# One-hots an expert ahead in bf16 and expert weights in chunk order, in a transformer block with expert-choice routing

## The chip, the cores and the metric

One core of a Trainium2 chip runs the whole block in one launch. The engines are TensorE (PE; its weight loads are listed as PEld), VectorE (DVE), ScalarE (ACT), GpSimd (POOL) and SyncE (SP, which here only issues transfers). The metric is the time of one execution on the device in microseconds. Three runs of the kernel before gave 1910.66, 1912.56 and 1914.64 us; their median is 1912.56 us.

## The reference

A diffusion-transformer block on 1024 tokens of width 1024, with 256 context tokens. It normalises and modulates the tokens, projects them, runs two attentions of 8 heads each (one over all tokens from a compressed latent, one over a local window), gates, projects and normalises again. Behind that comes the part that the change touches, a layer of 16 experts in which each expert chooses its tokens:

```
aff = softmax(u @ w_router)                  # 1024 tokens x 16 experts
g, idx = top_k(aff.T, 128)                   # each expert takes its 128 best tokens
xe = u[idx]                                  # 16 x 128 x 1024
h  = silu(xe @ w_exp_gate) * (xe @ w_exp_up) # 1024 x 1024 matrices per expert
ye = (h @ w_exp_down) * g
moe = zeros.at[idx].add(ye)                  # back to the tokens
out = layer_norm(ALPHA * x + g2 * moe)
```

Inputs and result are f32. The weights of the experts are 16 x 3 x 4 MB.

## The kernel before

Everything runs in an order written out by hand; each engine works through its instructions in that order and waits on semaphores. The attention, the projections and the normalisations come first and are left as they are. The expert stage begins at about 1206 us of the trace.

Each expert is a list of 12 chunks of weights (`units`, L1197): gate and up for two halves f of the hidden width and two halves q of the model width, then four chunks of down. A chunk is 1 MB and lies in one slot of a ring of 17 (`RB`, `slot_of_ring`); `load_next` (L1206) issues the next transfer on the SP queue as soon as a chunk has been used up. The source of a gate or up chunk is a block of 512 x 512 of the weight matrix, so a partition's 8 KB come as four runs of 2 KB; a down chunk comes as two runs of 4 KB.

To keep the precision of f32 with fast matmuls, each half chunk (128 x 1024) is split into a rounded high part on ScalarE (L1688) and the remainder on VectorE (L1689), at most four halves ahead of TensorE (`split_ahead`). Each product is then three matmuls of 512 columns (`mm3`, L90 to L92): 144 per expert. The expert's tokens and its hidden activations are transposed on TensorE in four groups of four 128 x 128 blocks (`transposed`, L1623) and split too (L1630, L1631). Expert 0 uses four of its chunks whole, in f32 matmuls (L1703).

The routing is done beside expert 0. `jobs` (from L1705) hangs small pieces of work on a place (expert, chunk i, quarter k). From the affinities come a threshold per expert (`highest`, `tau0` to `tau2`), masks and prefix sums (`pick0` to `pick2`), and then `slot`: for each token and expert its place among the expert's 128, or a value above 128.

To turn places into a list of tokens, the kernel builds one-hot matrices. For expert e and each of the 8 groups of 128 tokens, GpSimd compares a row 0..127 with the token's place (`onehot`, L1570); a 128 x 128 one-hot as the stationary operand, times a table `vals` of 17 f32 columns (token number and the 16 affinities), summed over the 8 groups in PSUM, gives each place its token and its gate (`summed`, L1575). There is room for four one-hots (`oh4`), so the work is in two parts:

```
def gather0(e):                      # at quarter k=0 of the chunk
    summed(found[e], oh4, vals, 0)
    onehot(slot[:, :, e], 4)
def gather1(e):                      # at quarter k=3
    summed(found[e], oh4, vals, 4)
    listed(e)                        # VectorE casts, GpSimd fetches the rows of u2
    if e < E - 1:
        onehot(slot[:, :, e + 1], 0)
```

`listed` (L1579) casts the sums to an index and a gate on VectorE (L1582, L1584) and starts an indirect transfer that fetches the 128 token rows (L1465). Expert 1's list is made in expert 0 (`onehot1`, `gather_first`, all 8 one-hots on VectorE), the lists of experts 2 and 3 in expert 1, and from then on the list of expert e in expert e - 2, at its chunk 2. At the end of an expert VectorE scales the output (L1787) and GpSimd adds it to the tokens' rows in memory by an indirect transfer (L1792). Beside expert 14, `order0` to `order2` work out an order of the rows for the end with the same one-hots. Behind the experts follow a normalisation and the output.

Of the kernel before, what the change touches and what calls it, by code (L numbers as in the profile page):

```python
# [9 lines left out]
F32 = mybir.dt.float32  # L10
F32R = mybir.dt.float32r
I32 = mybir.dt.int32
BF16 = mybir.dt.bfloat16
AF = mybir.ActivationFunctionType
OP = mybir.AluOpType
AX = mybir.AxisListType

T, L, D, H = 1024, 256, 1024, 8
N = T + L
KT = 8  # L20
E, CAP = 16, 128
# [6 lines left out]
def block_kernel(ctx, tc, a, out, dbg=None):  # L28

    nc = tc.nc  # L30
# [145 lines left out]
    with ExitStack() as st:  # L176
# [76 lines left out]
        for i in range(1, 4):  # L253
            k = 2 * i - 2
# [107 lines left out]
    o = {}  # L362
# [639 lines left out]
    with ExitStack() as st:  # L1002
# [39 lines left out]
        slot = kp.tile([128, 8, E], F32, name="slot")  # L1042
        col = kp.tile([128, 1], F32, name="col")
        flip = kp.tile([128, 128], F32, name="flip")
        onesr = kp.tile([128, 128], F32R, name="onesr")
        onesb = kp.tile([128, 128], BF16, name="onesb")
        idx0 = kp.tile([128, 1], I32, name="idx0")
        gg0 = kp.tile([128, 1], F32, name="gg0")
        gt = kp.tile([128, 9, E], F32R, name="gt")
        eq = kp.tile([128, 9, E], F32R, name="eq")  # L1050
        utr = kp.tile([128, 128], F32R, name="utr")
        er = kp.tile([128, 8, E], F32, name="er")
        tau = kp.tile([128, E], F32, name="tau")
        top = kp.tile([32, 128], F32, name="top")
        oh4 = kp.tile([128, 4, 128], F32, name="oh4")
        w0 = oh4[0:32].rearrange("p t c -> p (t c)")
        nst = ctx.enter_context(ExitStack())
        np_ = pool(nst, "rows", side="right")
        wr = np_.tile([128, KT, 32], F32, name="wr")
# [29 lines left out]
        def router():  # L1089
# [12 lines left out]
            lambda: rowload(sh2b, mod_d, 1),  # L1102
            lambda: (rowload(sc2b, mod_d, 2), nc.gpsimd.tensor_scalar(sc2b, sc2b, 1.0, None, op0=OP.add)),
            lambda: (nc.sync.dma_start(flip, a["flip"]), router()),
            lambda: (nc.sync.dma_start(col, a["col"]), nc.gpsimd.tensor_copy(onesr, ones),
                     nc.gpsimd.tensor_copy(onesb, ones)),
            lambda: (nc.gpsimd.memset(gt.bitcast(F32), 0.0), nc.gpsimd.memset(eq.bitcast(F32), 0.0),
                     nc.gpsimd.tensor_copy(utr, ut)),
        ]
        mhl, wo = {}, {}  # L1110
# [68 lines left out]
    def y_tile():  # L1179
        return xyp.tile([128, D], F32, name="ye")  # L1180
# [25 lines left out]
    def load_next(queue=nc.sync):  # L1206
        if pos[0] >= len(stream):
            return
        e, w, f, q = stream[pos[0]]
        raw = slot_of_ring()  # L1210
        if w == "down":
            r0 = f * 512 + q * 256
            src = a["w_exp_down"][e, r0:r0 + 256, :].rearrange("(k p) c -> p k c", p=128)
            queue.dma_start(raw.rearrange("p (k c) -> p k c", k=2), src)
        else:
            src = a["w_exp_" + w][e, q * 512:(q + 1) * 512, f * 512:(f + 1) * 512].rearrange("(k p) c -> p k c", p=128)
            queue.dma_start(raw.rearrange("p (k c) -> p k c", k=4), src)
        raws.append(raw.rearrange("p (k c) -> p k c", k=4))

    with ExitStack() as st:  # L1220
# [266 lines left out]
    with ExitStack() as st:  # L1487
# [7 lines left out]
        def bank(tag):  # L1495
            return psm.tile([128, 512], F32, name=tag)
# [45 lines left out]
        def prefix(m, q, first):  # L1542

            v = q.rearrange("p (t e) -> p t e", e=E)
            nc.tensor.matmul(v, utr, m, start=first, stop=False, skip_group_check=True)
            for t in range(8):
                nc.tensor.matmul(v[:, t + 1:9], onesr, m[:, t:t + 1].to_broadcast([128, 8 - t, E]),
                                 start=False, stop=(t == 7), skip_group_check=True)
            return v

        def pick1():
            q = bank("pY")
            vg = prefix(gt, q[:, 0:9 * E], True)
            vq = prefix(eq, q[:, 256:256 + 9 * E], False)
            nc.vector.tensor_copy(tau, vg[:, 8])
            nc.vector.tensor_tensor(er, vq[:, 0:8], tau[:, None, :].to_broadcast([128, 8, E]), op=OP.add)
            nc.vector.tensor_scalar(er, er, float(CAP), None, op0=OP.is_lt)
            eqf, gtf = eq.bitcast(F32)[:, 0:8], gt.bitcast(F32)[:, 0:8]
            nc.vector.tensor_tensor(er, er, eqf, op=OP.mult)
            nc.vector.tensor_tensor(gt[:, 0:8], gtf, er, op=OP.add)  # L1560

        def pick2():
            vs = prefix(gt, bank("pY")[:, 0:9 * E], True)
            nc.vector.tensor_scalar(er, gt.bitcast(F32)[:, 0:8], -1024.0, 1024.0, op0=OP.mult, op1=OP.add)
            nc.vector.tensor_tensor(slot, vs[:, 0:8], er, op=OP.add)

        def onehot(col, t0):

            for t in range(4):
                nc.gpsimd.tensor_scalar(oh4[:, t], iot, col[:, t0 + t:t0 + t + 1], None, op0=OP.is_equal)  # L1570

        def summed(pi, oh, what, t0):

            for t in range(t0, t0 + 4):
                nc.tensor.matmul(pi, oh[:, t - t0], what[:, t], start=(t == 0), stop=(t == 7))  # L1575

        found = {}

        def listed(e):  # L1579
            pi = found.pop(e)  # L1580
            idx = p.tile([128, 1], I32, name="idx", bufs=4)
            nc.vector.tensor_copy(idx, pi[:, 0:1])  # L1582
            gg = p.tile([128, 1], F32, name="gg", bufs=4)
            nc.vector.tensor_copy(gg, pi[:, 1 + e:2 + e])  # L1584
            xe = x_tile() if e % 2 else xe0
            fetch(xe, idx)
            got[e] = idx, gg, xe

        def gather0(e):
            found[e] = bank("pY")[:, :1 + E]  # L1590
            summed(found[e], oh4, vals, 0)
            onehot(slot[:, :, e], 4)

        def gather1(e):
            summed(found[e], oh4, vals, 4)
            listed(e)
            if e < E - 1:
                onehot(slot[:, :, e + 1], 0)

        ohs = []  # L1600

        def onehot1():
            oh = y_tile().rearrange("p (t c) -> p t c", c=128)
            nc.vector.tensor_tensor(oh, iot[:, None, :].to_broadcast([128, 8, 128]),
                                    slot[:, :, 1:2].to_broadcast([128, 8, 128]), op=OP.is_equal)
            ohs.append(oh)

        def gather_first():
            found[1] = bank("pY")[:, :1 + E]
            for t in (0, 4):  # L1610
                summed(found[1], ohs[0][:, t:], vals, t)
            listed(1)
            onehot(slot[:, :, 2], 0)

        def pair_of_parts():
            return [p.tile([128, 4, 128], F32R, name=n, bufs=3) for n in ("xh", "xl")]
# [95 lines left out]
        jobs[0, 7, 1] = [tau2]  # L1712
        jobs[0, 7, 3] = [pick0]
        jobs[0, 8, 1] = [pick1]
        jobs[0, 8, 3] = [pick2, onehot1]
        got = {}

        jobs[0, 9, 2] = [gather_first]
        for e in range(2, E):
            at = (1, 1) if e == 2 else (e - 2, 2 + 2 * (e == 3))  # L1720
            jobs[(*at, 0)] = [lambda e=e: gather0(e)]
            jobs[(*at, 3)] = [lambda e=e: gather1(e)]
        for k, job in ((8, order0), (24, order1), (30, order2)):
            jobs[(E - 2, *divmod(k + 4, 4))] = [job]
        got[0] = idx0, gg0, xe0
# [123 lines left out]
def _layout(inputs):  # L1849
# [3 lines left out]
    o = {}  # L1853
# [22 lines left out]
    for k in ("ln1_g", "ln1_b", "ln2_g", "ln2_b"):  # L1876
        o[k] = g[k]
    o["w_router"] = np.pad(g["w_router"][0].reshape(KT, 128, E).transpose(1, 0, 2), ((0, 0), (0, 0), (0, 32 - E)))
    for k in ("w_exp_gate", "w_exp_up", "w_exp_down"):
        o[k] = g[k][0]  # L1880
    rb = np.pad(g["na_rel_bias"][0].reshape(H * 15, 31), ((0, 0), (48, 48)))
    o["rb"] = np.tile(rb, (1, 64))

# [41 lines left out]
```

## Time and profile before

| What | us |
|---|---|
| Median of three runs | 1912.56 |
| Profiled execution, its own time | 1914.66 |
| Span of that execution, first to last instruction | 1912.9 |
| PE busy | 1747.6 (91%) |
| DVE busy | 1197.5 (63%) |
| ACT busy | 939.8 (49%) |
| POOL busy | 671.0 (35%) |
| L1689, DVE, remainders of the expert weights, first group, 183 instructions | 222.9 |
| L1570, POOL, one-hots, 112 instructions | 125.2 |

The span is the profiled execution without 1.8 us around it. Busy times of PE count matmuls that overlap each other, so its share says little about how close it is to its limit; what one matmul costs is seen from start to start. The rows used further on come from windows, from lists of waits and from timelines. In a timeline a row has its start, its length, the engine, the line, what is written from what, and in brackets the idle time before it and what ended it. Line numbers are those of the kernel before.

### The profile page before, as it was taken

To read this page: it belongs to the slowest core of one execution; us is meant where nothing else is said; L and a number is where in the kernel's file an instruction comes from. 1 tells how busy PE (TensorE), PEld (TensorE's weight loads), DVE (VectorE), ACT (ScalarE), POOL (GpSimd) and SP (SyncE) were. 2 spreads that over 40 slices of the span, in tenths; PEclk is the share of its full clock that TensorE was granted. 3 is DMA by queue.
4 is the path that set the end of the run, shared out by engine and by line. 5 is a ranking of instruction groups with operands and counts; after the bars stand their busy time and mean duration, and the time that the engine had idled before them with its cause. 6 is when DMAs were issued, how large, how long until landed. Compare 5 with 4: busy or idle time off the path is not lost.

```text
span 1912.9 us, 25632 instructions
## 1 busy us (share of the span) xinstructions
PE 1747.6 (91%) x9751; PEld 1391.9 (73%) x9753; DVE 1197.5 (63%) x1827; ACT 939.8 (49%) x1479; POOL 671.0 (35%) x529
## 2 busy tenths in 40 slices
PE   5999999999899899999998887799999999999993
PEld 3788778888788777777676665477777777777772
DVE  5612331121777665565544888868888778888887
ACT  3422222111677665666610322446666666666675
POOL 1344545540334231120043555652223332222134
PEclk9999999999999999999999999799999999999996
DMA  7334554264343211000155436789999999999953
GB/s 308 117 106 139 211 199 142 78 167 132 77 87 75 58 31 27 20 19 1 56 171 180 174 143 238 289 274 321 331 332 328 315 344 334 330 334 330 321 186 130
DMA packets 153722, 356.63 MB, mean 186 GB/s; under 512 B 28368, under 2 KB 36944, under 8 KB 152320
## 3 DMA queue, kind: packets, MB, share of 16 engines
q1 hardware_dynamic: 134320, 283.68, 44.2%
q0 software_dynamic: 11920, 43.52, 7.6%
q10 hardware_dynamic: 7360, 27.81, 3.7%
q8 instruction: 76, 1.25, 0.3%
q14 instruction: 46, 0.38, 0.1%
HBM read 312.85 MB, written 42.12 MB: 186 GB/s over the span
## 4 chain that ended last, share of the span: by engine, by line
PE 66%; DVE 11%; POOL 8%; DMA 6%; issue 4%; ACT 3%; SPq 1%; ACTq 0%; DVEq 0%; POOLq 0%
PE pS L401 10%; PE pY L921 4%; DMA rawm<-in_w_mod_dram 4%; PE pT L894 4%; PE pup L90 3%; PE pup L91 3%; PE pup L92 3%; PE pD L90 3%; PE pD L92 3%; PE pD L91 3%; POOL oh L1570 3%; PE pgate L90 3%; PE pgate L92 3%; PE pgate L91 2%; DMA raw<-in_w_proj_dram 2%
## 5 line engine op out<-in xcount | busy, mean ns | idle before, releaser
L1689 DVE TENSOR_TENSOR hl<-raw,hl 128x1024 fp32r<-128x1024 f32 x183 | 222.9, 1245 | 60.0 <-ACT hl L1688 59.4
L1688 ACT ACTIVATE hl<-raw 128x1024 fp32r<-128x1024 f32 x188 | 193.9, 1056 | 96.1 <-PE pgate L92 63.6
L1792 POOL DMA_INDIRECT acc_d<-ye,idx x15 | 35.3, 2355 | 372.0 <-DVE ye L1787 372.0
L401 PE MATMUL pS<-uhi,whi 128*128 128x512 f32 (+1 forms) x440 | 131.3, 387 | 3.0 <-DVE stg L488 2.4
L87 DVE TENSOR_TENSOR wlo<-raw,whi 128x1024 fp32r<-128x1024 f32 x25 | 37.2, 1492 | 148.4 <-ACT whi L86 148.4
L1570 POOL TENSOR_SCALAR oh<-iot,slot 128x128 f32<-128x128 f32 x112 | 125.2, 1132 | 11.7 <-PE pY L1575 11.1
L401 PE MATMUL pS<-uhi,wlo 128*128 128x512 f32 (+1 forms) x440 | 129.1, 382 | 0.0
L401 PE MATMUL pS<-ulo,whi 128*128 128x512 f32 (+1 forms) x440 | 129.1, 382 | 0.0
L1688 ACT ACTIVATE whl<-raw 128x1024 fp32r<-128x1024 f32 x94 | 99.7, 1060 | 51.5 <-PE pgate L92 36.6
L1689 DVE TENSOR_TENSOR whl<-raw,whl 128x1024 fp32r<-128x1024 f32 x91 | 111.2, 1222 | 16.6 <-ACT whl L1688 16.4
L306 POOL TENSOR_TENSOR sb<-qs,sa 128x512 fp32r<-128x512 f32 x28 | 35.9, 1282 | 240.3 <-DVE sa L305 109.5
L1689 DVE TENSOR_TENSOR raw<-raw 128x1024 fp32r<-128x1024 f32 x92 | 112.2, 1220 | 11.4 <-ACT raw L1688 11.4
L905 ACT ACTIVATE pt<-pT 128x512 f32<-128x512 f32 x128 | 69.7, 595 | 95.4 <-PE pT L894 95.1
L1688 ACT ACTIVATE raw<-raw 128x1024 fp32r<-128x1024 f32 x94 | 99.5, 1058 | 27.9 <-PE pup L92 17.4
L376 POOL TENSOR_TENSOR rawm<-rawm,scol 128x1024 f32<-128x1024 f32 x32 | 63.6, 1989 | 135.1 <-DMA rawm<-in_w_mod_dram 135.1
L880 DVE TENSOR_REDUCE sn<-pS 128x1 f32<-128x1024 f32 x64 | 78.3, 1223 | 40.5 <-PE pS L92 40.3
L1237 PE MATMUL pS<-raw,hl 128*128 128x512 f32 x384 | 98.0, 404 | 2.3 <-DVE t L1151 2.2
L401 PEld LDWEIGHTS pS<-uhi,whi 128*128 128x128 f32 x440 | 79.2, 189 | 22.9 <-issue 3.0
L894 PE MATMUL pT<-ident,pm 128*128 128x128 f32 x640 | 94.5, 279 | 1.2 <-ACT pt L905 1.0
L921 PE MATMUL pY<-pt,v 128*64 128x256 f32 x640 | 84.1, 395 | 10.5 <-ACT inv L721 10.5
L401 PEld LDWEIGHTS pS<-ulo,whi 128*128 128x128 f32 x440 | 80.3, 189 | 16.4
L401 PEld LDWEIGHTS pS<-uhi,wlo 128*128 128x128 f32 x440 | 80.3, 189 | 16.2
(478 smaller groups left out, 4860.4 us busy)
## 6 DMA issues: line engine op xcount, KB each, us to landing
raw<-in_w_exp_down_dram SPq DMA_DIRECT2D x64, 1024.0 KB
raw<-in_w_exp_gate_dram SPq DMA_DIRECT2D x63, 1024.0 KB
raw<-in_w_exp_up_dram SPq DMA_DIRECT2D x63, 1024.0 KB
rawm<-in_w_mod_dram POOLq DMA_DIRECT2D x32, 512.0 KB, 3.9
raw<-in_w_in_dram SPq DMA_DIRECT2D x25, 512.0 KB
wm<-in_w_mod_dram SPq DMA_DIRECT2D x8, 1024.0 KB
sig_d<-stg ACTq DMA_DIRECT2D x16, 512.0 KB
sg<-sig_d SPq DMA_DIRECT2D x32, 256.0 KB
```

The source lines that it names most:

```text
L90: nc.tensor.matmul(ps, ahi, bhi, start=first, stop=False)
L91: nc.tensor.matmul(ps, ahi, blo, start=False, stop=False)
L92: nc.tensor.matmul(ps, alo, bhi, start=False, stop=last)
L401: nc.tensor.matmul(pt[:, c0:c1], ww[:, kt], uu[:, kt, c0:c1], start=(kt == 0 and k == 0), stop=(kt == KT - 1 and k == 2))
L880: nc.vector.tensor_reduce(sm[:, 0:1], ps, axis=AX.X, op=OP.max)
L894: nc.tensor.transpose(tb[b][:, (k - k0) * 128:(k - k0 + 1) * 128], Pm[n][:, k * 128:(k + 1) * 128], ident)
L905: nc.scalar.activation(dst, src, AF.Copy)
L921: nc.tensor.matmul(py[0][h * 64:(h + 1) * 64, 0:256], vm[:, k, col:col + 64], PT[g, h][:, k], start=(k == 0), stop=(k == 9))
L1237: nc.tensor.matmul(ps[b], x[:, kt], w[:, kt % 4], start=(kt == 0 and k == 0), stop=(kt == 7 and k == 2))
L1570: nc.gpsimd.tensor_scalar(oh4[:, t], iot, col[:, t0 + t:t0 + t + 1], None, op0=OP.is_equal)
L1688: nc.scalar.activation(w[:, 0], src, AF.Copy)
L1689: lo_on(e, i).tensor_tensor(w[:, 1], src, w[:, 0].bitcast(F32), op=OP.subtract)
```

## The change

It has three parts.

The one-hots and the table become bf16. Eight of them fit where four f32 ones lay (`ohb`, a view of `oh4`). A token number and an affinity don't fit in one bf16 value, so `values` builds, once, a table `v5` of five bf16 columns per token and expert: two whose sum is the token number and three whose sum is the affinity. The masks of the prefix sums and the matrices that they are multiplied with become bf16 too. Sums over the columns are taken by VectorE behind the matmuls.

The one-hots of expert e + 1 are all made right after the gather of expert e, and the second part of the gather moves from quarter k=3 to k=2. The separate functions for expert 1 go.

The arrays of expert weights are handed over in another order: each chunk is one contiguous block in which every partition's 8 KB lie together, so that a load is one plain transfer.

```diff
-        gt = kp.tile([128, 9, E], F32R, name="gt")
-        eq = kp.tile([128, 9, E], F32R, name="eq")
-        utr = kp.tile([128, 128], F32R, name="utr")
+        gt = kp.tile([128, 9, E], BF16, name="gt")
+        eq = kp.tile([128, 9, E], BF16, name="eq")
+        utr = kp.tile([128, 128], BF16, name="utr")
...
+        ohb = oh4.rearrange("p t c -> p (t c)").bitcast(BF16).rearrange("p (t c) -> p t c", t=8)
+
+        v5 = kp.tile([128, 8, E, 5], BF16, name="v5")
...
-        if w == "down":
-            r0 = f * 512 + q * 256
-            src = a["w_exp_down"][e, r0:r0 + 256, :].rearrange("(k p) c -> p k c", p=128)
-            queue.dma_start(raw.rearrange("p (k c) -> p k c", k=2), src)
-        else:
-            src = a["w_exp_" + w][e, q * 512:(q + 1) * 512, f * 512:(f + 1) * 512].rearrange("(k p) c -> p k c", p=128)
-            queue.dma_start(raw.rearrange("p (k c) -> p k c", k=4), src)
+        queue.dma_start(raw, a["w_exp_" + w][e, f, q])
...
-                nc.tensor.matmul(v[:, t + 1:9], onesr, m[:, t:t + 1].to_broadcast([128, 8 - t, E]),
+                nc.tensor.matmul(v[:, t + 1:9], onesb, m[:, t:t + 1].to_broadcast([128, 8 - t, E]),
...
-        def listed(e):
-            pi = found.pop(e)
+        def values():
+
+            tok = vals[:, :, 0:1].to_broadcast([128, 8, E])
+            nc.vector.tensor_scalar(v5[:, :, :, 0], tok, col, None, op0=OP.subtract)
+            nc.vector.tensor_tensor(v5[:, :, :, 1], tok, v5[:, :, :, 0], op=OP.subtract)
+            x = aff
+            for k in range(2, 5):
+                nc.vector.tensor_copy(v5[:, :, :, k], x)
+                if k < 4:
+                    nc.vector.tensor_tensor(er, x, v5[:, :, :, k], op=OP.subtract)
+                    x = er
+
+        def onehots(e):
+
+            for t in range(8):
+                nc.gpsimd.tensor_scalar(ohb[:, t], iot, slot[:, t, e:e + 1], None, op0=OP.is_equal)
+
+        def gather(e, part):
+
+            if part == 0:
+                found[e] = bank("pY")[:, :5]
+            pi = found[e]
+            for t in range(4 * part, 4 * part + 4):
+                nc.tensor.matmul(pi, ohb[:, t], v5[:, t, e], start=(t == 0), stop=(t == 7))
+            if part == 0:
+                return
             idx = p.tile([128, 1], I32, name="idx", bufs=4)
-            nc.vector.tensor_copy(idx, pi[:, 0:1])
+            at = p.tile([128, 1], F32, name="tokat", bufs=4)
+            nc.vector.tensor_reduce(at, pi[:, 0:2], axis=AX.X, op=OP.add)
+            nc.vector.tensor_copy(idx, at)
             gg = p.tile([128, 1], F32, name="gg", bufs=4)
-            nc.vector.tensor_copy(gg, pi[:, 1 + e:2 + e])
+            nc.vector.tensor_reduce(gg, pi[:, 2:5], axis=AX.X, op=OP.add)
             xe = x_tile() if e % 2 else xe0
             fetch(xe, idx)
             got[e] = idx, gg, xe
...
+            if e + 1 < E:
+                onehots(e + 1)
...
-            oh = y_tile().rearrange("p (t c) -> p t c", c=128)
-            nc.vector.tensor_tensor(oh, iot[:, None, :].to_broadcast([128, 8, 128]),
+            nc.vector.tensor_tensor(ohb, iot[:, None, :].to_broadcast([128, 8, 128]),
                                     slot[:, :, 1:2].to_broadcast([128, 8, 128]), op=OP.is_equal)
...
-        jobs[0, 8, 3] = [pick2, onehot1]
+        jobs[0, 8, 3] = [pick2, onehot1, values]
         got = {}
 
-        jobs[0, 9, 2] = [gather_first]
+        jobs[0, 9, 2] = [lambda: gather(1, 0), lambda: gather(1, 1)]
         for e in range(2, E):
             at = (1, 1) if e == 2 else (e - 2, 2 + 2 * (e == 3))
-            jobs[(*at, 0)] = [lambda e=e: gather0(e)]
-            jobs[(*at, 3)] = [lambda e=e: gather1(e)]
+            jobs[(*at, 0)] = [lambda e=e: gather(e, 0)]
+            jobs[(*at, 2)] = [lambda e=e: gather(e, 1)]
...
-    for k in ("w_exp_gate", "w_exp_up", "w_exp_down"):
-        o[k] = g[k][0]
+    for k in ("w_exp_gate", "w_exp_up"):
+        o[k] = g[k][0].reshape(E, 2, 4, 128, 2, 512).transpose(0, 4, 1, 3, 2, 5).reshape(E, 2, 2, 128, 2048)
+    o["w_exp_down"] = g["w_exp_down"][0].reshape(E, 2, 2, 2, 128, D).transpose(0, 1, 2, 4, 3, 5).reshape(E, 2, 2, 128, 2048)
```

The lines that move data between f32 and f32r views of the masks go with their types; `order0` to `order2` keep their f32 one-hots.

## Rows read from the trace of the kernel before

**Rows 1.** Busy time by window (us from the start), granted clock, DMA share, GB/s.
```profile
1550.00:1590.00 40.00, 38.43 (x171) 30.84 (x170) 32.60 (x34) 27.47 (x30) 13.12 (x10) 0.96 0.96 331
```
**Rows 2.** Timeline of PE: first matmul of experts 1, 2, 14, 15; the last.
```profile
1264.19 0.50 PE L90 MATMUL pgate<-whl,xh 128*128 128x512 f32 x1 [0.25 <-ACT xh L1630]
...
1310.74 0.40 PE L90 MATMUL pgate<-whl,xh 128*128 128x512 f32 x1
...
1805.48 0.40 PE L90 MATMUL pgate<-whl,xh 128*128 128x512 f32 x1
...
1845.05 0.40 PE L90 MATMUL pgate<-whl,xh 128*128 128x512 f32 x1
...
1879.42 0.39 PE L92 MATMUL pD<-raw,xl 128*128 128x512 f32 x1
```
**Rows 3.** Line L1575, what PE sat idle for before it (us, times).
```profile
  POOL oh L1570: 52.9, 96
```
**Rows 4.** Timeline of PE around the gather in expert 8.
```profile
1564.22 0.40 PE L92 MATMUL pup<-raw,xl 128*128 128x512 f32 x1
1564.46 0.96 PE L1575 MATMUL pY<-vals,oh 128*128 128x17 f32 x8
...
1565.59 0.40 PE L91 MATMUL pgate<-whl,xh 128*128 128x512 f32 x1
...
1567.23 0.39 PE L92 MATMUL pgate<-hl,xl 128*128 128x512 f32 x1
...
1570.93 0.40 PE L91 MATMUL pgate<-hl,xh 128*128 128x512 f32 x1
```
**Rows 5.** Window behind that gather, columns as in rows 1.
```profile
1572.00:1575.30 3.30, 3.30 (x10) 2.60 (x9) 1.55 (x2) 2.08 (x3) 3.26 (x5) 0.52 1.03 416
```
**Rows 6.** Timeline of PE around a group of four transposes.
```profile
1501.71 0.40 PE L92 MATMUL pgate<-hl,xl 128*128 128x512 f32 x1
1501.95 0.60 PE L1623 MATMUL pY<-ident,hs 128*128 128x128 f32 x4
...
1502.63 0.40 PE L91 MATMUL pup<-hl,xh 128*128 128x512 f32 x1
```
**Rows 7.** POOL: one-hots (min/median/max ns; mean in 1330 to 1800 us), one fetch.
```profile
L1570 POOL TENSOR_SCALAR oh<-iot,slot x112: 590/622/2710, 1258.2 to 1775.3; 128x128 f32<-128x128 f32 x112
...
L1570 POOL TENSOR_SCALAR oh<-iot,slot 128x128 f32<-128x128 f32 x84 | 93.9, 1131 | 8.4 <-PE pY L1575 8.0
...
1274.15 1.06 POOL L1465 DMA_INDIRECT xe<-u_d,idx  x1 [0.93 <-DVE gg L1584]
```
**Rows 8.** Timeline of expert 0: a small DVE operation, DVE's one-hots, the first gather.
```profile
1249.71 0.29 DVE L1559 TENSOR_TENSOR er<-er,eq 128x128 f32<-128x128 f32 x1
...
1252.65 1.23 DVE L1604 TENSOR_TENSOR ye<-iot,slot 128x1024 f32<-128x1024 f32 x1
...
1254.11 1.85 PE L1575 MATMUL pY<-vals,ye 128*128 128x17 f32 x16
```
**Rows 9.** One group of splits on DVE, 1330 to 1800 us: busy us, mean ns, idle before.
```profile
L1689 DVE TENSOR_TENSOR hl<-raw,hl 128x1024 fp32r<-128x1024 f32 x138 | 166.8, 1236 | 44.7 <-ACT hl L1688 44.2
```
**Rows 10.** DMA queues, 1330 to 1800 us: packets, MB, share of 16 engines.
```profile
q1 hardware_dynamic: 60579, 143.94, 86.8%
q0 software_dynamic: 3168, 11.54, 9.4%
```
**Rows 11.** Two windows as in rows 1, and an issue before 25 us.
```profile
20.00:30.00 10.00, 1.71 (x7) 1.32 (x8) 7.96 (x20) 4.39 (x4) 2.50 (x2) 1.00 1.01 426
...
1831.00:1838.00 7.00, 7.00 (x38) 5.88 (x37) 5.30 (x7) 5.02 (x7) 0.07 (x1) 1.00 0.20 81
...
wm<-in_w_mod_dram SPq DMA_DIRECT2D x4, 1024.0 KB
```
**Rows 12.** Timeline of expert 0: two splits side by side, on POOL and DVE.
```profile
1236.46 2.35 POOL L1689 TENSOR_TENSOR hl<-raw,hl 128x1024 fp32r<-128x1024 f32 x1
...
1236.88 3.00 DVE L1689 TENSOR_TENSOR hl<-raw,hl 128x1024 fp32r<-128x1024 f32 x1 [1.85 <-ACT hl L1688]
```

More of the change, by code (lines that the diff above doesn't have):

```diff
@@ L1044, in block_kernel @@
         flip = kp.tile([128, 128], F32, name="flip")
-        onesr = kp.tile([128, 128], F32R, name="onesr")
         onesb = kp.tile([128, 128], BF16, name="onesb")
@@ L1104, in block_kernel @@
             lambda: (nc.sync.dma_start(flip, a["flip"]), router()),
-            lambda: (nc.sync.dma_start(col, a["col"]), nc.gpsimd.tensor_copy(onesr, ones),
-                     nc.gpsimd.tensor_copy(onesb, ones)),
-            lambda: (nc.gpsimd.memset(gt.bitcast(F32), 0.0), nc.gpsimd.memset(eq.bitcast(F32), 0.0),
+            lambda: (nc.sync.dma_start(col, a["col"]), nc.gpsimd.tensor_copy(onesb, ones)),
+            lambda: (nc.gpsimd.memset(gt, 0.0), nc.gpsimd.memset(eq, 0.0),
                      nc.gpsimd.tensor_copy(utr, ut)),
@@ L1557, in pick1 @@
             nc.vector.tensor_scalar(er, er, float(CAP), None, op0=OP.is_lt)
-            eqf, gtf = eq.bitcast(F32)[:, 0:8], gt.bitcast(F32)[:, 0:8]
-            nc.vector.tensor_tensor(er, er, eqf, op=OP.mult)
-            nc.vector.tensor_tensor(gt[:, 0:8], gtf, er, op=OP.add)
+            nc.vector.tensor_tensor(er, er, eq[:, 0:8], op=OP.mult)
+            nc.vector.tensor_tensor(gt[:, 0:8], gt[:, 0:8], er, op=OP.add)
         def pick2():
             vs = prefix(gt, bank("pY")[:, 0:9 * E], True)
-            nc.vector.tensor_scalar(er, gt.bitcast(F32)[:, 0:8], -1024.0, 1024.0, op0=OP.mult, op1=OP.add)
+            nc.vector.tensor_scalar(er, gt[:, 0:8], -1024.0, 1024.0, op0=OP.mult, op1=OP.add)
             nc.vector.tensor_tensor(slot, vs[:, 0:8], er, op=OP.add)
@@ L1587, in listed @@
             got[e] = idx, gg, xe
[L1589 to L1600, printed above, removed]
+            if e + 1 < E:
+                onehots(e + 1)
         def onehot1():
-            oh = y_tile().rearrange("p (t c) -> p t c", c=128)
-            nc.vector.tensor_tensor(oh, iot[:, None, :].to_broadcast([128, 8, 128]),
+            nc.vector.tensor_tensor(ohb, iot[:, None, :].to_broadcast([128, 8, 128]),
                                     slot[:, :, 1:2].to_broadcast([128, 8, 128]), op=OP.is_equal)
[L1606 to L1613, printed above, removed]
         def pair_of_parts():
```

## The prediction

> **What bounds the kernel now.** I read the busy times by windows first. In the middle of the expert stage TensorE is busy 38.4 of 40 us, VectorE 32.6 and the DMA engines 96% [rows 1], so three resources stand near their limit and the question is which of them sets the pace. Next the timeline of TensorE, for the first matmul of each expert: expert 1 takes 1310.74 - 1264.19 = 46.55 us, experts 2 to 13 take (1805.48 - 1310.74) / 12 = 41.23 us each, and expert 15, from 1845.05 to its last matmul at 1879.42, takes 34.4 us with the same 144 big matmuls [rows 2]. Expert 15 has no gather of a later expert in it. The reader is to see that an expert without a gather costs 7 us less, although it streams the same weights through the same engines: neither the weights nor VectorE set the 41 us.
>
> Then the waits of the gather's line: TensorE stood idle 52.9 us for the one-hots of GpSimd (L1570), 96 times [rows 3], and there is no other entry of that size in the stage. The timeline around one gather puts a price on it. A big matmul's pitch comes from expert 15: (1879.42 - 1845.05 - 2 x 0.45) / 143 = 0.234 us (0.45 is a group of four transposes, below). From the matmul at 1564.22 to that at 1565.59 lie two pitches and the first half of the gather: 1.37 - 0.47 = 0.90 us. From 1567.23 to 1570.93 lie two pitches and the second half: 3.70 - 0.47 = 3.23 us, of which 1.6 us is waiting for GpSimd and the rest thin matmuls that arrive between the waits [rows 4]. Right behind it the granted clock is 0.52 for 3.3 us [rows 5], so nearly all of it at 1.2 GHz instead of 2.4: 3.3 x 0.48 = 1.6 us lost. TensorE had just been through the thin, waiting second half; the first half, which does not wait, is followed by no fall.
>
> An expert without any of this: 144 x 0.234 = 33.7 us, and four groups of four transposes at (1502.63 - 1501.71) - 0.47 = 0.45 us each [rows 6], together 35.5 us. Check: 35.5 + 0.90 + 3.23 + 1.6 = 41.2, the period seen. So TensorE in program order, with one wait and one clock fall per expert, is the bound.
>
> **The change part by part.**
>
> *One-hots an expert ahead.* GpSimd now makes all 8 one-hots of expert e+1 right after the gather of e, and TensorE asks for them one expert later. Eight at 1.13 us (mean; 0.59 at least, 2.71 at most) and the indirect fetch of 1.06 us make 10.1 us of GpSimd's queue [rows 7], with the scatter-add behind them, in an expert of over 36 us. The 1.6 us wait goes; I count the clock fall as gone too, since its only neighbour is that wait (if it stays: rival B).
>
> *Thin matmuls in bf16.* Before, each half is 4 f32 matmuls that appear as 8 records [rows 4]. After, it is 4 bf16 matmuls of 5 columns. No row shows this operation. Ends: nothing, and the 0.90 us of the f32 half. I take 0.45 us, the four single-record transposes with a 128x128 weight load each [rows 6], the nearest rows. New expert: 35.5 + 2 x 0.45 = 36.4 us.
>
> Experts 2 to 13: 12 x (41.23 - 36.4) = 58.0 us.
>
> *Expert 1* holds two gathers. New: 35.5 + 4 x 0.45 = 37.3, and the 0.3 us wait at its start stays. Expert 3's one-hots have no whole expert of cover: after the gather of 2 GpSimd needs about 0.5 us for VectorE's index (0.93 us wait in the row), 1.06 and 8 x 1.13 = 10.6 us, while TensorE is back at the second half after 1.4 + 5.6 + 0.45 + 1.4 = 8.9 us (two half chunks, two chunks, the first half): a wait of 1.7 us. 46.55 - 39.3 = 7.2 us gained. Ends of that wait: 0, and 1.7 + 1.6 with a clock fall.
>
> *Expert 0.* The gather of expert 1, 16 records from 1254.11, shrinks from about 1.8 to 0.9 us. But its operands now come from VectorE in order: the one-hots end at 1252.65 + 1.23 = 1253.9, and then stand 7 small operations of the new value table, at up to 0.29 us each by a 128x128 row of the same stage, some 1.8 us [rows 8]. TensorE, there at 1254.1, waits until 1255.7. Queued behind them on VectorE are the low parts of the next hidden chunk and two weight halves, which TensorE wants more than 1.5 us later. Net 0.7 us lost. The prefix matmuls in bf16 I count as nothing: they are 27 thin ones in all, run once.
>
> *The second half moves from k=3 to k=2* of its chunk. Cast, fetch and one-hots move with it by one k, some 0.7 us, past nothing on the SP queue; two small reductions for one copy cost VectorE below 0.3 us an expert, hidden as long as it is not the bound.
>
> *VectorE* has 32.6 x 41.1/40 = 33.5 us of work per expert [rows 1], for 36.4 us: 92%. A split takes 1.236 us on average [rows 9], against 1.23 for the one-hot instruction of the same shape, which ran with nothing on GpSimd [rows 8]: the one-hots that run beside some of the splits now hardly stretch them. When the wait goes, VectorE is the next engine late. I take 0.2 us of TensorE per expert for it, 13 experts: 2.5 us lost. Ends: 0 and the 1.9 us of rival D.
>
> *Chunk-wise weights.* A gate or up chunk is now read in runs of 2 KB, a down chunk in 4 KB, after the change in 8 KB. Now the weights' queue moves 143.94 MB in 86.8% of 470 us, 353 GB/s while it has the engines, and the indirect queue takes 9.4% [rows 10]: 12.58 / 0.353 = 35.6 and 3.9 us, 39.5 us per expert, more than the new expert. In the 20 to 30 us window, with the modulation weights in 8 KB runs among 4 KB ones, the engines moved 426 GB/s [rows 11]: 29.5 + 3.9 = 33.4 us, less than 36.4. By the Trainium skill ("DMA: Bandwidth & Descriptors", Specifications) runs from 512 B on are already at line rate; by that rule the new layout would give nothing, and these rows do not agree with it: 353 against 426 GB/s. TensorE does not wait for a load now, so this part earns no time by itself; it keeps the transfers off the path, and the ring is a second cover (rival A).
>
> **Sum.** 58.0 + 7.2 - 0.7 - 2.5 = 62 us. The profiled execution took 1914.66 us, 2.1 above the median of 1912.56, and would take 1852.7; against the median the forecast is **1851 us**. Its own range is 1842 to 1864: with the halves at 0.90 us it is 12 us later, at nothing 12 earlier (I allow 9), and the waits of experts 0 and 1 move it by 3 either way.
>
> **Rivals.**
>
> *D: VectorE becomes the bound through GpSimd.* For: when a GpSimd split of 2.35 us ran beside it, a VectorE split took 3.00 instead of 1.24 us [rows 12], and one-hots of 2.71 us show that they wait too. After the change all eight run beside a full VectorE. If each holds a split for its own 0.6 us, VectorE needs 33.5 + 8 x 0.6 = 38.3 us, and so does the expert: 13 x 1.9 = 25 us later, 1876. Against: the split's mean of 1.236 us, which contains such neighbours already. The Trainium skill ("SBUF — State Buffer", SBUF: two separate sides) has GpSimd and VectorE take turns on a shared port pair, the loser standing still for a whole instruction, also where VectorE reads two SBUF inputs; the 3.00 us row agrees, and by that rule this rival is the outcome to expect wherever the one-hots come first.
>
> *B: the clock still falls once per expert,* because the two halves are thin work even without a wait: 13 x 1.6 = 21 us, 1872. Against: no fall behind the first half today.
>
> *A: the loads become the bound.* If the layout gives nothing, the loads need 39.5 against 36.4 us: 13 x 3.1 = 40 us behind. But the engines fall to a 20% share from 1831 us on [rows 11], 48 us before the last matmul; that lead would nearly all be eaten and nothing lost. With half of the lead, 1869.
>
> *C: the one-hots are not ahead,* their writes held back until the wait is as before; only the bf16 halves remain: 13 x 0.9 = 12 us gained, 1900.
>
> *E, slower than before.* VectorE overrun by one-hots of the longest kind: 8 x 2.71 = 21.7 us per expert in which a split takes 3.00 us. It finishes 7.2 splits there instead of 17.5, loses 10.3 x 1.236 = 12.7 us, and the expert takes 46.2: 13 x 5.0 = 65 us slower, 1978. It decides from 7.7 us lost per expert on. For it speaks only that both durations occur; against it, that the median one-hot takes 0.62 us.
>
> **How the numbers follow.** Forecast 0.70, D 0.13, B 0.06, A 0.04, C 0.03, E 0.03, no change 0.01. The range 1842 to 1876 takes in the forecast's own, B, A and the milder part of D, and leaves out C, E and the tails. A measurement of this kernel tells about 0.2% (4 us) from no change: faster 0.96, same 0.01, slower 0.03.
>
> **What would show it.** Right: no wait for GpSimd at the gather from expert 2 on, a period of 36.2 to 36.8 us, a granted clock of 1.0 through experts 2 to 13, a weights queue above 400 GB/s while it has the engines. A period of 38 us with matmuls waiting for VectorE's low parts is D; a 0.5 clock once per expert is B; ACT starting splits late behind loads is A. The forecast is wrong if the period stays above 37.5 us or the time above 1876.

## The result and the profile after

The kernel after takes 1848.47 us in the median, beside 1911.61 us for the kernel before on the same chip: a ratio of 0.967 (95%: 0.964 to 0.969). Forecast were 1851 us and 1842 to 1876. One of the four executions, of 3365.91 us, was a slow one; it counts in the median but not in the ratio, and the other three took 1846.82 to 1849.55 us. The profiled execution took 1849.55 us with a span of 1847.8, against 1914.66 and 1912.9 before: 65.1 us of span are gone. A ratio below stands against the kernel before as it ran beside that run.

The timeline of TensorE after the change, cut to the starts of experts 1, 2, 14 and 15, the last matmul, one gather in the middle (in expert 8) and the waits that the text speaks of (columns as in rows 2):

```profile
1212.90 1.08 PE L1624 MATMUL pY<-ident,xe 128*128 128x128 f32 x4 [8.13 <-DMA xe<-u_d,idx]
...
1256.07 0.35 PE L1597 MATMUL pY<-v,oh 128*128 128x5 bf16 x8 [2.87 <-DVE v L1581]
1256.28 0.48 PE L90 MATMUL pD<-raw,xh 128*128 128x512 f32 x1
...
1266.52 0.63 PE L1624 MATMUL pY<-ident,xe 128*128 128x128 f32 x4 [2.99 <-DMA xe<-u_d,idx]
...
1267.84 0.50 PE L90 MATMUL pgate<-whl,xh 128*128 128x512 f32 x1 [0.25 <-ACT xh L1631]
...
1282.82 0.18 PE L1597 MATMUL pY<-v,oh 128*128 128x5 bf16 x1 [1.22 <-POOL oh L1589]
1284.47 0.18 PE L1597 MATMUL pY<-v,oh 128*128 128x5 bf16 x1 [1.47 <-POOL oh L1589]
...
1310.50 0.40 PE L90 MATMUL pgate<-whl,xh 128*128 128x512 f32 x1
...
1529.91 0.40 PE L91 MATMUL pup<-raw,xh 128*128 128x512 f32 x1
1530.14 0.40 PE L92 MATMUL pup<-raw,xl 128*128 128x512 f32 x1
1530.38 0.26 PE L1597 MATMUL pY<-v,oh 128*128 128x5 bf16 x4
1530.50 0.48 PE L90 MATMUL pgate<-whl,xh 128*128 128x512 f32 x1
1530.82 0.40 PE L91 MATMUL pgate<-whl,xh 128*128 128x512 f32 x1
...
1739.06 0.40 PE L90 MATMUL pgate<-whl,xh 128*128 128x512 f32 x1
...
1761.39 1.03 PE L1570 MATMUL pY<-vals,oh 128*128 128x8 f32 x8 [1.90 <-DVE xl L1632]
...
1780.06 0.40 PE L90 MATMUL pgate<-whl,xh 128*128 128x512 f32 x1
...
1814.30 0.40 PE L92 MATMUL pD<-raw,xl 128*128 128x512 f32 x1
```

Experts 2 to 13 take (1739.06 - 1310.50) / 12 = 35.71 us each, where they took 41.23 [rows 2]. The thin half at 1530.38 costs 0.91 us from one big matmul to the third behind it, less three pitches of 0.234: about 0.2 us, where it was 0.90 [rows 4]. The whole span is accounted for by stretches of [rows 2] and of this fence:

| Stretch | Before, us | After, us | Gain, us | Forecast, us |
|---|---|---|---|---|
| up to expert 1 | 1264.19 | 1267.84 | -3.65 | -0.7 |
| expert 1 | 46.55 | 42.66 | 3.9 | 7.2 |
| experts 2 to 13 | 494.74 | 428.56 | 66.2 | 58.0 |
| expert 14 | 39.57 | 41.00 | -1.4 | 0 |
| expert 15 to the end | 67.85 | 67.74 | 0.1 | 0 |
| VectorE's share | | | 0 | -2.5 |

So the total came out near the forecast partly by luck, through errors that offset each other: 8.2 us better in the middle and 2.5 us that VectorE did not take, against 7.6 us worse around the middle.

Windows after the change, columns as in rows 1: the middle, all of experts 2 to 13 with what lies just beside them, and the three stretches of low clock from expert 1 on that a wait precedes.

```profile
1510.00:1550.00 40.00, 40.00 (x188) 32.10 (x187) 37.60 (x41) 31.71 (x36) 14.98 (x12) 1.00 0.99 386
...
1299.00:1762.00 463.00, 461.11 (x2167) 369.88 (x2165) 438.16 (x463) 358.19 (x388) 166.15 (x120) 1.00 1.00 381
...
1268.10:1271.50 3.40, 3.40 (x9) 2.39 (x9) 3.40 (x5) 1.95 (x3) 0.79 (x1) 0.52 0.04 14
...
1285.20:1288.60 3.40, 3.40 (x13) 2.39 (x12) 0.74 (x1) 1.06 (x1) 1.53 (x3) 0.52 1.03 433
...
1763.10:1766.50 3.40, 3.40 (x10) 2.61 (x9) 0.96 (x1) 1.54 (x2) 1.49 (x3) 0.51 0.61 245
```

In the middle TensorE is busy 40.00 of 40 us, VectorE 37.6, and the DMA engines are at 99%; the granted clock is 1.00 through 463 us, where it fell once per expert [rows 5]. The three falls left stand right behind waits in the timeline: the 2.99 us at 1266.52, the 1.47 at 1284.47, the 1.90 at 1761.39.

What TensorE sat idle for before the gather's line, now L1597 (us, times; loads and matmuls together). The entry that held 52.9 us in 96 waits [rows 3] holds 6.1 in 5, and VectorE's value table stands beside it:

```profile
  DVE v L1581: 6.2, 2
  POOL oh L1589: 6.1, 5
```

Groups of instructions from 1310 to 1730 us, columns as in rows 9: GpSimd's one-hots and the largest group of VectorE's splits. The split's mean was 1236 ns before [rows 9].

```profile
L1690 DVE TENSOR_TENSOR hl<-raw,hl 128x1024 fp32r<-128x1024 f32 x142 | 170.5, 1228 | 12.5 <-ACT hl L1689 10.6
...
L1589 POOL TENSOR_SCALAR oh<-iot,slot 128x128 bf16<-128x128 f32 x88 | 109.0, 1254 | 0.4
```

DMA queues from 1310 to 1730 us, columns as in rows 10: 147.46 / (0.876 x 420) = 401 GB/s while the weights' queue has the engines, where it was 353.

```profile
q1 hardware_dynamic: 20244, 147.46, 87.6%
```

### The profile page after: what moved, and what is told of

The parts are those of the page before. It is cut to its first block, busy times and chain, and to the rows that moved or that the text cites. A ratio compares the mean times of both kernels' runs of the same rounds, so it can differ in the third digit from the quotient of the medians.

```text
span 1847.8 us, 25506 instructions
## 1 busy us (share of the span) xinstructions
PE 1693.6 (92%) x9633; PEld 1344.2 (73%) x9633; DVE 1202.8 (65%) x1849; ACT 939.4 (51%) x1479; POOL 688.2 (37%) x528
## 4 chain that ended last, share of the span: by engine, by line
PE 66%; DVE 12%; DMA 7%; POOL 7%; issue 3%; ACT 3%; SPq 1%; ACTq 0%; POOLq 0%; DVEq 0%
PE pS L401 10%; PE pY L921 4%; DMA rawm<-in_w_mod_dram 4%; PE pT L894 4%; PE pgate L90 3%; PE pD L90 3%; PE pD L92 3%; PE pD L91 3%; PE pup L90 3%; PE pup L91 3%; PE pup L92 3%; PE pgate L92 3%; PE pgate L91 3%; DMA raw<-in_w_proj_dram 2%; PE pS L90 2%
## 5 line engine op out<-in xcount | busy, mean ns | idle before, releaser
L87 DVE TENSOR_TENSOR wlo<-raw,whi 128x1024 fp32r<-128x1024 f32 x25 | 37.6, 1508 | 148.6 <-ACT whi L86 148.5
L1589 POOL TENSOR_SCALAR oh<-iot,slot 128x128 bf16<-128x128 f32 x112 | 133.2, 1204 | 0.5
L1690 DVE TENSOR_TENSOR raw<-raw 128x1024 fp32r<-128x1024 f32 x92 | 112.4, 1222 | 6.6 <-ACT raw L1689 6.6
```

The costliest lines, as they stand in the source:

```text
L1589: nc.gpsimd.tensor_scalar(ohb[:, t], iot, slot[:, t, e:e + 1], None, op0=OP.is_equal)
L1690: lo_on(e, i).tensor_tensor(w[:, 1], src, w[:, 0].bitcast(F32), op=OP.subtract)
```

## The experiments

The theory: the wait for GpSimd and the clock fall behind it were the price of the gather; with the one-hots an expert ahead TensorE's own work is the bound, and the chunk layout keeps the loads from becoming it. Its rivals are D (one-hots hold VectorE), B (thin work makes the clock fall, wait or not) and a layout that does something else, or nothing.

**The layout alone, on the kernel before.**

```diff
+        queue.dma_start(raw, a["w_exp_" + w][e, f, q])
...
+    for k in ("w_exp_gate", "w_exp_up"):
+        o[k] = g[k][0].reshape(E, 2, 4, 128, 2, 512).transpose(0, 4, 1, 3, 2, 5).reshape(E, 2, 2, 128, 2048)
```

> The kernel before with the chunk-wise weights alone. Theory (the layout only keeps the loads off the path): no change, 1908 to 1914 us, experts 2 to 13 still 41.1 us each, the wait for the one-hots and one clock fall per expert as before; the weights' queue moves about 400 GB/s instead of 353 while it has the engines and takes some 76% of the time instead of 87%. Rival (the faster loads carry part of the 63 us): below 1900 us with a shorter period.

Measured: 1915.23 us, ratio 1.0024 (1.0014 to 1.0034). It is a little slower. Experts 3 to 13 still take 41.1 us each with their wait and their fall. So the layout alone earns nothing. The expectation missed in one point: the weights' queue did not speed up to 400 GB/s. From 1330 to 1700 us, columns as in rows 10:

```profile
q1 hardware_dynamic: 15525, 113.03, 83.9%
```

113.03 / (0.839 x 370) = 364 GB/s in runs of 8 KB, where the kernel before moves 352 in the same window.

**The whole change without the layout.** The same hunks taken back.

> The kernel after with the weights in their old order, so in runs of 2 and 4 KB. Theory (the ring's lead of some 48 us covers the loads' deficit of 39.5 - 35.7 = 3.8 us per expert, 13 x 3.8 = 49 us in all): 1848 to 1858 us, a period of 35.7 us until the last two or three experts, DMA share 1.0. Rival (loads are the bound as soon as the wait is gone): the period is 39.5 us from expert 2 on, 1848 + 13 x 3.8 = 1897 us. Second rival (the layout doesn't matter at all): 1848 us and free DMA time.

Measured: 1844.04 us, ratio 0.9657 (0.9643 to 0.9671); the kernel after had 0.9667 in its runs and 0.9685 (0.9667 to 0.9702, 1850.05 us) in a repeat beside the last three experiments. TensorE's timeline, first matmuls of experts 2 and 14:

```profile
1303.79 0.40 PE L90 MATMUL pgate<-whl,xh 128*128 128x512 f32 x1
...
1732.35 0.40 PE L90 MATMUL pgate<-whl,xh 128*128 128x512 f32 x1
```

The weights' queue from 1330 to 1700 us, columns as in rows 10:

```profile
q1 hardware_dynamic: 55682, 130.93, 92.9%
```

(1732.35 - 1303.79) / 12 = 35.71 us, to the last expert. The runs of 2 and 4 KB move 130.93 / (0.929 x 370) = 381 GB/s when the kernel asks for them that fast. The 353 GB/s of [rows 10] was what a kernel of 41 us per expert asked for, not what its runs could do. At the same pace the 8 KB runs are only 3 to 5% faster (364 against 352 GB/s in experts of 41 us; 401 against 381 in experts of 35.7 us). Rival A was false by more than its lead: there was nothing to keep off the path, and the lead was not used up either, for the engines fall idle some 48 us before the last matmul here and 49 us with the layout. Nearest comes the second rival, that the layout doesn't matter; the time is 4 us below even that, and there is no free DMA time (a share of 1.04 from 1510 to 1550 us).

**The wait put back, with the thin work still in bf16.** One-hots 4 to 7 are made only after the first half, the second half stands at k=3 again.

```diff
-            for t in range(8):
+            for t in range(t0, t0 + 4):
...
+                if e > 1:
+                    onehots(e, 4)
...
-                onehots(e + 1)
+                onehots(e + 1, 0)
```

> The kernel after, still in bf16, but the last four one-hots of an expert are made only after the first half of its gather, and the second half stands at k=3 again, as before the change. Theory (the wait and the clock fall behind it are most of the gain): four one-hots at 1.2 us from the first half on, TensorE back after 2.1 us, so a wait of 2.7 us and one clock fall of 1.6 us per expert: a period of 40.0 us, 1848 + 13 x 4.3 = 1904 us. Rival (the thin matmuls in bf16 carry the gain): 1850 to 1860 us. Third (the wait comes back but the clock does not fall): 1848 + 13 x 2.7 = 1883 us and a granted clock of 1.0 in experts 2 to 13.

Measured: 1888.88 us, ratio 0.9903 (0.9882 to 0.9924), between the 1904 us of the theory and the 1883 us of the third expectation, a wait without a fall. TensorE's timeline, starts of experts 3, 4 and 5 and two of the waits back in expert 3:

```profile
1344.66 0.40 PE L90 MATMUL pgate<-whl,xh 128*128 128x512 f32 x1
...
1354.92 0.18 PE L1597 MATMUL pY<-v,oh 128*128 128x5 bf16 x1 [1.12 <-POOL oh L1589]
1355.49 0.18 PE L1597 MATMUL pY<-v,oh 128*128 128x5 bf16 x1 [0.40 <-POOL oh L1589]
...
1384.79 0.40 PE L90 MATMUL pgate<-whl,xh 128*128 128x512 f32 x1
...
1423.33 0.40 PE L90 MATMUL pgate<-whl,xh 128*128 128x512 f32 x1
```

Windows right behind the waits of experts 3 and 4, columns as in rows 1:

```profile
1356.40:1359.80 3.40, 3.40 (x10) 2.62 (x9) 1.23 (x1) 1.84 (x2) 2.96 (x3) 0.50 1.01 413
1395.60:1399.00 3.40, 3.39 (x16) 2.77 (x17) 1.61 (x4) 2.04 (x3) 2.04 (x2) 1.00 1.01 367
```

Expert 3 takes 40.13 us and has the fall (clock 0.50); expert 4 takes 38.54 with the same waits and has none. Of experts 2 to 13 six take 40.1 and six 38.55. The wait brings the fall but not each time; the fall costs 40.12 - 38.55 = 1.57 us, as the forecast had it (1.6), and this wait 38.55 - 35.71 = 2.84 us.

**The one-hots ahead in f32, with 17 columns, no value table.**

```diff
-                nc.gpsimd.tensor_scalar(ohb[:, t], iot, slot[:, t, e:e + 1], None, op0=OP.is_equal)
+                nc.gpsimd.tensor_scalar(ohf(t), iot, slot[:, t, e:e + 1], None, op0=OP.is_equal)
...
-                nc.tensor.matmul(pi, ohb[:, t], v5[:, t, e], start=(t == 0), stop=(t == 7))
+                nc.tensor.matmul(pi, ohf(t), vals[:, t], start=(t == 0), stop=(t == 7))
```

> The kernel after with one-hots an expert ahead, but in f32 with the table of 17 columns as before, in eight buffers of which two are reused small tiles; the bf16 value table is left out. Theory (thin f32 halves cost 0.9 us each where bf16 ones cost 0.2, and the wait alone made the clock fall): a period of 35.7 + 1.4 = 37.1 us, 13 x 1.4 = 18 us later less the value table's 2.9 us wait: 1863 us, granted clock 1.0 in experts 2 to 13. Rival (thin f32 work makes the clock fall even without a wait): one fall per expert more, 1863 + 13 x 1.6 = 1884 us.

Measured: 1859.59 us, ratio 0.974 (0.972 to 0.976). First matmuls of experts 2 and 14, then a window over what lies between them:

```profile
1303.83 0.40 PE L90 MATMUL pgate<-whl,xh 128*128 128x512 f32 x1
...
1749.27 0.40 PE L90 MATMUL pgate<-whl,xh 128*128 128x512 f32 x1
```

```profile
1304.00:1771.00 467.00, 465.74 (x2200) 380.38 (x2199) 423.72 (x439) 348.78 (x377) 171.46 (x117) 1.00 0.99 367
```

445.44 / 12 = 37.12 us per expert, clock 1.00 throughout: the same thin f32 matmuls that stood before a fall in every expert bring none when nothing waits. Rival B is false. bf16 in the gather is worth 37.12 - 35.71 = 1.4 us per expert, and the order (no wait, no fall) 41.23 - 37.12 = 4.1. The order here takes in the move of the second half from k=3 to k=2, which no run tries by itself; the chunk layout is in this kernel too, but the first experiment shows that it earns nothing.

**Each one-hot of experts 4 to 15 made twice.**

```diff
-            for t in range(8):
+            for t in [t for t in range(8) for _ in range(1 + (e > 3))]:
```

> The kernel after with each one-hot of experts 4 to 15 made twice on GpSimd, 16 per expert, some 20 us of its queue in an expert of 35.7 us. Theory (GpSimd has the cover and does not hold VectorE): period 35.7 us, 1848 us, splits on VectorE still 1.23 us. Rival D (each one-hot holds a split for 0.6 us): 8 x 0.6 = 4.8 us more work for VectorE, which is busy 95% already: a period of 38 to 40 us, 1880 us or more.

Measured: 1847.1 us, ratio 0.9677 (0.9659 to 0.9695); experts 2 to 13 at 35.70 to 35.74. A window in the middle, and the one-hots' group from 1310 to 1730 us:

```profile
1510.00:1550.00 40.00, 40.00 (x190) 32.15 (x189) 37.78 (x40) 31.02 (x34) 32.38 (x23) 1.00 1.00 387
```

```profile
L1589 POOL TENSOR_SCALAR oh<-iot,slot 128x128 bf16<-128x128 f32 x176 | 268.9, 1536 | 8.7
```

GpSimd is busy 32.4 of 40 us instead of 15.0, VectorE 37.8 instead of 37.6, and TensorE never waits. A one-hot takes 1536 ns, with a least of 590 [rows 7]: where the two meet, GpSimd is the one that is stretched (VectorE's largest group of splits has a mean of 1222 ns). Rival D is false, and with it E.

**The three losses around the middle, mended.** The values move to GpSimd and earlier; the gather of expert 3 moves from chunk 4 to 7 of expert 1; `order1` and `order2`, which delay VectorE before TensorE's wait in expert 14, move by two k.

```diff
-            nc.vector.tensor_scalar(v5[:, :, :, 0], tok, col, None, op0=OP.subtract)
+            nc.gpsimd.tensor_scalar(v5[:, :, :, 0], tok, col, None, op0=OP.subtract)
...
-        jobs[0, 8, 3] = [pick2, onehot1, values]
+        jobs[0, 6, 3].append(values)
+        jobs[0, 8, 3] = [pick2, onehot1]
...
-            at = (1, 1) if e == 2 else (e - 2, 2 + 2 * (e == 3))
+            at = (1, 1) if e == 2 else (e - 2, 2 + 5 * (e == 3))
...
-        for k, job in ((8, order0), (24, order1), (30, order2)):
+        for k, job in ((8, order0), (26, order1), (32, order2)):
```

> The kernel after with its three remaining waits in experts 0, 1 and 14 taken away: the value table is made on GpSimd, which is idle then, and four chunks earlier; the gather of expert 3 stands three chunks later, so that GpSimd has finished its one-hots; the last two steps of the final order stand two quarters later. Theory (each wait is on the path, and those in experts 1 and 14 bring a clock fall behind them): 2.9 + (2.7 + 1.6) + (1.9 + 1.6) = 10.7 us, 1838 us, ratio 0.961. Rival (the waits only hide others, such as the fetch for expert 1 that lands late): 1843 us or more, with a longer wait for the token rows at the start of expert 1.

Measured: 1838.82 us, ratio 0.963 (0.9617 to 0.9643), beside 1850.05 for the kernel after. TensorE's timeline at the value table, at the rows of expert 1, in expert 1 and in expert 14:

```profile
1251.41 0.36 PE L1597 MATMUL pY<-v,oh 128*128 128x5 bf16 x8 [0.33 <-DVE oh L1613]
...
1262.11 0.70 PE L1624 MATMUL pY<-ident,xe 128*128 128x128 f32 x4 [3.24 <-DMA xe<-u_d,idx]
...
1286.70 0.24 PE L1597 MATMUL pY<-v,oh 128*128 128x5 bf16 x4 [1.41 <-DVE xl L1632]
...
1753.29 0.92 PE L1570 MATMUL pY<-vals,oh 128*128 128x8 f32 x7 [0.49 <-DVE xl L1632]
```

The wait for the values fell from 2.87 to 0.33 us, expert 1 from 42.5 to 38.9, expert 14 from 41.0 to 38.1. The three places are losses of the table, as read. A fourth stays: TensorE waits 3.24 us for the rows of expert 1, with a low clock behind it (2.99 us in the kernel after), although the value table no longer stands in VectorE's way.

**The same without the layout.** 

> The same as the three waits removed, but with the weights in their old order. Theory (runs of 8 KB make the indirect transfers beside them land later: fetches 7.3 us against 5.2 for the first, and the ring covers the slower loads): the first fetch lands after 5.2 us, 2 to 4 us faster than the same kernel with chunk-wise weights, 1834 us, ratio 0.959. Rival (the layout was neutral and the difference between the two single runs came from the stages before): no difference, ratio within 0.001 of the kernel with chunk-wise weights.

Measured: 1836.43 us, ratio 0.9619 (0.9605 to 0.9634), the lowest of all. It lies 2.4 us under the run before it, with intervals that overlap; the direction is that of the two layout runs above. The first fetch landed after 6.2 us, not 5.2, and the ratios differ by 0.0011, so this run doesn't decide between its theory and its rival.

## Why the prediction was right, and which steps were off

*What bounds the kernel: right.* TensorE in program order was the bound: it is so still, at 40.00 of 40 us, and what the gather cost in waits and clock went. Of the signs named, the missing waits (rival C is out with them), the clock of 1.0 and a weights' queue above 400 GB/s came (the last is not why the time fell, see the layout); the period of 35.71 us lies below the 36.2 to 36.8 us that were named. With the order alone changed (f32 ahead) 4.1 of the 5.5 us per expert come; bf16 brings the rest.

*Thin halves in bf16: mis-sized.* 0.45 us was taken from transposes of 128 columns; the half of four measured 0.2. Two halves in twelve experts: 6 us more gained. The bounds, 0 and 0.90, held it. The middle gained 2.2 us more than that; 1.45 us of it lie in expert 6 of the kernel before, which took 42.56 us where the others took 41.1, with a clock of 0.50 from 1486.5 to 1493.2 us, twice as long as behind the other gathers.

*VectorE's 2.5 us: nothing.* It is 94% busy in the middle, its splits take 1.22 to 1.24 us as before, and TensorE does not wait for them. By the Trainium skill ("SBUF — State Buffer", SBUF: two separate sides) VectorE and GpSimd take turns on a shared port pair, and whichever comes second stands. The traces show it on GpSimd's side (one-hots of 1.25 and 1.54 us against a least of 0.59), and none of the loss on VectorE's that rival D needs.

*Expert 1: mechanism right, size off.* Forecast was 39.3 us, measured 42.66. The wait for the one-hots of expert 3 is there, 1.22 + 1.47 = 2.7 us instead of 1.7; two falls, at 1268.1 and 1285.2, cost about 3.4 x 0.48 = 1.6 us each: the second was in the bounds of that wait, the first, behind the wait for the rows (below), was nowhere; the four halves gave 1.0 back. 39.3 + 1.0 + 3.2 - 1.0 = 42.5.

*Expert 0: this step failed.* From the gather to expert 1 it forecast a net loss of 0.7 us; measured were 4.6. The value table was put at 1.8 us of VectorE; its first and last operation and the split behind it in VectorE's timeline are

```profile
1253.46 0.40 DVE L1577 TENSOR_SCALAR v<-vals,col 128x128 bf16<-128x128 f32 x1
...
1255.67 0.34 DVE L1581 CAST v<-er 128x128 bf16<-128x128 f32 x1
...
1259.06 1.22 DVE L1690 TENSOR_TENSOR raw<-raw 128x1024 fp32r<-128x1024 f32 x1
```

2.55 us, and TensorE waits 2.87. That the splits queued behind it were not wanted yet was right, but the forecast stopped there and did not follow the fetch of expert 1's rows, which comes behind the index of the gather. It goes out at 1259.32 instead of 1257.18, 6.1 us after TensorE came to the gather (3.1 before), and it takes longer. GpSimd's timeline:

```profile
1259.32 1.84 POOL L1461 DMA_INDIRECT xe<-u_d,idx  x1 [19.59 <-DVE gg L1605]
```

It stands beside VectorE's split of 1259.06. In the kernel before VectorE then waited for ScalarE, and the fetch took 1.03 us. TensorE's wait of 2.99 us at 1266.52 is this fetch, and no step had it. It is not the layout's: without the layout it is 3.30 us. Nor is it the value table's: with the table on GpSimd and made earlier (the three losses mended) the fetch takes 1.86 us and TensorE waits 3.24. In the f32 kernel, which sums its lists in f32 like the kernel before, VectorE stands idle for ScalarE as the fetch goes out; it takes 1.01 us and TensorE doesn't wait for it. That the bf16 gather, 1.5 us shorter on TensorE (0.21 against 1.70 us without the wait), brings ScalarE and with it the split forward onto the fetch fits all these traces; no run changes that alone. Two fetches of the kernel after show the same: 1.98 us at 1277.03 beside a split, 1.02 us at 1289.62 with VectorE idle. The same page of the Trainium skill has an operation of VectorE in a two-port mode keep GpSimd from writing such a transfer's descriptors, but infers that tensor_tensor, which the splits are, leaves that writing alone. The traces don't agree with it: 1.84 to 1.86 us beside a split against 1.01 and 1.03 with VectorE idle. The measurement decides, and why the issue is longer stays open.

Over the whole kernel, the fetch's own line and its time from issue to landing, after and then before:

```profile
L1461 POOL DMA_INDIRECT xe<-u_d,idx x16: 1019/1496/1977, 1205.4 to 1714.1; - x16
...
DMA to landing us min/median/max: 4.5/9.3/9.6
```

```profile
L1465 POOL DMA_INDIRECT xe<-u_d,idx x16: 1011/1042/1100, 1206.0 to 1776.8; - x16
...
DMA to landing us min/median/max: 4.4/6.4/7.8
```

From 1330 to 1700 us the median landing is 6.1 us with the layout alone and 8.2 with all but the layout: so the later fetches of the middle come with the new experts and not with the layout. The longer issue is not the reason: in the f32 kernel the fetches of the middle are issued in 1.03 us and land after 9.9. Where it arises is open. In the middle the fetch has an expert of time, so it costs nothing there.

In sum, against before: the first transposes of expert 0 start 1.5 us later (the layout in part, below), the gather with its wait takes 3.08 us instead of 1.70, from there to expert 1 it is 11.56 us instead of 8.38, and between first transposes and gather expert 0 is 2.4 us shorter (40.30 against 42.72): -1.5 - 1.4 - 3.2 + 2.4 = -3.7. Of these 2.4 us, 1.95 lie where the 27 prefix matmuls stand, which the forecast put at nothing. TensorE's timeline from the first of them to the next transposes, before and after:

```profile
1246.81 0.23 PE L1545 MATMUL pY<-gt,utr 128*128 128x144 f32 x1
...
1252.26 0.60 PE L1623 MATMUL pT<-ident,hs 128*128 128x128 f32 x4
```

```profile
1247.70 0.24 PE L1541 MATMUL pY<-gt,utr 128*128 128x144 bf16 x1
...
1251.20 0.60 PE L1624 MATMUL pT<-ident,hs 128*128 128x128 f32 x4
```

That is 5.45 against 3.50 us. With the layout alone, where the masks are still f32, it is 5.45 too; with the one-hots in f32 but the masks in bf16, 3.50.

*The layout: wrong.* That "it keeps the transfers off the path" rested on taking the rate that a kernel used for the rate that it could get. The Trainium skill ("DMA: Bandwidth & Descriptors", Specifications) has runs from 512 B on at line rate, and the forecast held 353 against 426 GB/s against it; the run without the layout decides for that rule as far as the time goes. Some microseconds seem even lost by it: 0.24% on the kernel before, clear of the noise; 4 to 6 us between the medians with and without it on the kernel after, with intervals that overlap. Part of that may be the first fetch of expert 0, which lands after 7.2 us with the layout alone and 5.1 without it in the kernel after, so that TensorE waits 8.02 instead of 6.02 us in the one pair, 8.13 instead of 5.90 in the other; but in the last pair it is 8.03 against 7.81, and in the repeat of the kernel after 10.13. Where the rest is lost stays open: the stages before differ between executions by as much. Rival A's figure with half of the lead was mis-added: 1851 + 40 - 24 gives 1867 us, not 1869; nothing rests on it.

*Expert 14: missed.* The wait of 1.90 us for VectorE at 1761.39 was there before (1.86 us), but then no fall followed, as the window behind it in the kernel before shows (columns as in rows 1):

```profile
1829.40:1832.80 3.40, 3.40 (x16) 2.75 (x15) 1.25 (x2) 2.34 (x3) 1.67 (x3) 1.00 0.86 342
```

After the change the clock there is 0.51 for 3.4 us, and the expert takes 1.4 us more. Why the same wait brings a fall in some kernels and none in others stays open. Taking 1.4 us off that wait took the fall with it: 38.1 us.

## What to carry to other kernels

An operand that the bounding engine waits for is worth more than its wait: on TensorE the half-clock stretch that may follow comes on top, and moving the producer one iteration ahead removes both, even where the work itself stays as slow. A queue's rate in a trace can be what the kernel asked for, as here (353 GB/s became 381 with the same runs); as long as TensorE is not seen waiting for a load, no layout should be priced by it. Where a change moves a chain at the start of a stage (values, index, fetch, transposes), follow the chain to its last link: TensorE's wait of 3 us for the first rows stood in no step, and it stayed when the new work in front of it was taken away. What the steady middle covers, the first iterations pay.

## What the runs showed of the hardware that was not expected

- The clock fall is not a fixed price of a wait: with the same waits of 0.9, 1.1 and 0.4 us it came in six of twelve experts, and behind the wait of 1.9 us in expert 14 in five of the eight profiles that have it.
- Four bf16 matmuls of 5 columns, each with a 128x128 weight load, cost 0.2 us between big matmuls; f32 ones of 17 columns cost 0.9 (twice that difference is the 1.4 us per expert between the two kernels).
- VectorE at 94% beside a GpSimd at 81% lost nothing measurable, while GpSimd's 0.59 us instruction took 1.54 us on average.
- The issue of an indirect fetch took 1.5 to 2.0 us beside a split of VectorE and 1.0 us with VectorE idle. How late it lands does not follow from that: 9.3 us in the median with issues of 1.5 us, 9.9 in the middle of the f32 kernel with issues of 1.03.
- The stretch with the 27 prefix matmuls, of at most 144 columns, took 1.95 us less of TensorE's time in bf16 than in f32 (3.50 against 5.45).
